# Four 64 by 64 quarters in place of full products with zero blocks, in the state-space part of a decoder layer

## Chip, cores and metric

The kernel runs on one core of one Trainium2 chip. The metric is the device time of one execution in microseconds (us), as the median of the runs.

## What is computed

One layer of a hybrid decoder for 264 columns: 256 prompt tokens and 8 sample tokens. In the mixing part, 16 attention heads and 64 state-space groups both read the same input product; their outputs are normed and go through `w_out`; a gated feed-forward part and a last gated addition follow. The change is in the state-space groups:

```
_, _, s_re, s_im = lax.associative_scan(_cplx_combine, (a_seq_re, a_seq_im, bu_re, bu_im), axis=1)
...
y = (jnp.einsum('ntgp,gcp->ntgc', s_re, prm['ssm_c_re'].astype(f32))
     - jnp.einsum('ntgp,gcp->ntgc', s_im, prm['ssm_c_im'].astype(f32))
     + prm['ssm_d'].astype(f32) * uf)
z = jnp.einsum('ntgc,gce->ntge', jax.nn.gelu(y), prm['ssm_w_glu'].astype(f32))
out = z[..., :SSM_CH_GROUP] * jax.nn.sigmoid(z[..., SSM_CH_GROUP:])
```

A group has 16 channels and a complex state of 64 numbers.

## The kernel before

**The stream.** All large weights come in units of 1024 columns (`w_load`, L336). ScalarE rounds a unit to `wh` (`w_high`, L349), VectorE forms the rest `wl` (`w_low`, L357), and TensorE makes three products of 128 by 128 by 264 columns for each block of 128 by 128: `acc<-xh,wh`, `acc<-xl,wh`, `acc<-xh,wl`. The phases are, in order: `in` (the input product), `oa` and `os` (the attention's and the state-space half of `w_out`), `pp`, `gu`, `dn`, `pg` (`stream`, L1519). The attention (`attn`, L544) and the state-space groups are worked off while `in` and `oa` are streamed; `os` needs the normed state-space output, and nothing of the stream may go ahead of it.

**Attention.** Eight steps of two heads: scores `s<-kt,q`, reductions on VectorE, exponentials and scaling on ScalarE, transposes `pt<-ident,s`, copies `ptt`, product `o<-ptt,vnat`, copies `aops` and squares `sqa`, sum `ssq_a`. `ps_a` is the product that adds up `ssq_a` for the norm (`attn_norm`, L704).

**State space.** The 64 groups are worked in 8 eighths `e` of 4 pairs `g`, with the pair's two groups `h` in the two halves of 64 partitions. Time is cut into 32 blocks of 8 tokens: inside a block the effect of the input is a product with a table `T`, and from block to block a scan runs. For each eighth:

- `ssm_x` (L950) forms tables, `px`, `ph`, `p2`, and sends `t7` through DRAM (`td`) into `T`.
- `ssm_w` (L1015) makes `pw` (8 products, 64 columns of the array each) for the scan and `py<-T,U` (8 of the same kind), which opens the sums in the bank `py`. Then `ws`, transposes `pw<-ident,ws`, copies `wt`, and on VectorE `rt`, the scan `rsh`, and the state `SB`.
- `SB` has, for each pair and each of real and imaginary part, a 128 by 128 square: group 0 in rows and columns 0 to 63, group 1 in 64 to 127, zeros in the other two quarters.
- `ssm_y` (L1098) adds the state's part, `py<-G,SB`: 4 pairs times 2 parts, 8 full products of 128 by 128 with the zeros, into `py`. Then the gelu `gy`, four transposes `py<-ident,gy`, a copy `yt`, and the transfer `ys` to DRAM.
- `ssm_glu` (L1127), eight times: transfers `wg` and `gt`, products `zb` and `za` (the gated product), `sg`, `so`, `sops` and the sum of squares `ssq_s`. There is one buffer of `gt` and `wg`. `ps_s` (`ssm_norm`, L1167) adds up `ssq_s` and stands ahead of the `os` products.

**What sets the order.** A planner (`Pace`, L76) runs all these steps as generators with costs in us and counted buffers ("+bk:2" takes two banks of `bk`), and records them in the order that it finds; up to the `os` phase a scheduler of the framework orders the instructions of each engine again. An engine then works in its fixed order. There are 8 PSUM banks: 3, later 2, are for `acc`, the others are `bk`. `py` holds one from `ssm_w` to `ssm_y`.

Every float32 product is two records in the trace. `mm` is L285, transposes are L289, ScalarE's instructions L281, DMA issues L296.

Of the kernel before, what the change touches and what calls it, by code (L numbers as in the profile page):

```python
# [12 lines left out]
ACTF = mybir.ActivationFunctionType  # L13
# [3 lines left out]
P = 128  # L17
D = 2048
KD = D // P
T = 264  # L20
# [177 lines left out]
def build(nc, tc, ctx, a):  # L198
    pace = Pace()
    V, S, G, PE, SP = nc.vector, nc.scalar, nc.gpsimd, nc.tensor, nc.sync  # L200

    def size(ap):
        n = 1
        for x in ap.shape[1:]:
            n *= x
        return n
# [17 lines left out]
    def mul(out, in0, in1):  # L224
        tt(out, in0, in1, ALU.mult)

    def add(out, in0, in1):
        tt(out, in0, in1, ALU.add)

    def sub(out, in0, in1):  # L230
        tt(out, in0, in1, ALU.subtract)
# [29 lines left out]
    def pcopy(out, in_, scale=None):  # L261
        pace.use("pool", 0.5 + 1.0e-3 * size(out))
        if scale is None:
            G.tensor_copy(out=out, in_=in_)
        else:
            G.tensor_scalar(out=out, in0=in_, scalar1=scale, scalar2=None, op0=ALU.mult)
# [5 lines left out]
    def act(out, in_, func=ACTF.Copy, **kw):  # L272
        own = {ACTF.Exp: 1, ACTF.Tanh: 1, ACTF.Gelu_apprx_tanh: 2, ACTF.Sigmoid: 3, ACTF.Silu: 4,
               ACTF.Abs_reciprocal_sqrt: 5}.get(func)
        if own and own != pace.table and not (func == ACTF.Tanh and pace.table in (1, 2, 3, 4)):
            pace.table = own
            pace.use("act", 1.28)

        own = sum(hasattr(kw.get(n), "tensor") for n in ("scale", "bias", "accum_out"))
        pace.use("act", 0.09 + 0.093 * own + 0.833e-3 * size(out))  # L280
        S.activation(out=out, in_=in_, func=func, **kw)  # L281

    def mm(out, lhsT, rhs, cost, start=True, stop=True):
        pace.use("pe", cost)
        PE.matmul(out, lhsT, rhs, start=start, stop=stop)  # L285

    def tr(out, in_, ident):
        pace.use("pe", 0.11)
        PE.transpose(out, in_, ident)  # L289

    def dma(out, in_):
        n = 4.0
        for x in out.shape:
            n *= x
        pace.move(n)
        SP.dma_start(out=out, in_=in_)  # L296
# [20 lines left out]
    def bank(shape, name):  # L317
        return banks.tile(shape, F32, tag="bank", name=name)
# [610 lines left out]
    def gsl(e):  # L929
        return slice(4 * e, 4 * e + 4)  # L930

    XT, HG, PY = {}, {}, {}
# [82 lines left out]
    def ssm_w(e):  # L1015
        q, hf = e // 2, e % 2
        u = U2[e % 2]
        gs = slice(4 * hf, 4 * hf + 4)
        yield "sp", [f"us{q}", f"us{q + 4}"] + ([f"U{e - 2}"] if e > 1 else ["c_zero"])
        for h in range(2):  # L1020
            c = q + 4 * h
            dma(u[:, 4 * h:4 * h + 4, :], us[c].rearrange("j c g k -> (j c) g k")[:, gs, :])
        yield "pe", [f"XT{e}", f"T{e}", "+bk:2"]
        pw = bank([P, 4, P], "pw")
        xt = XT.pop(e)
        for g in range(4):
            for h in range(2):
                mm(pw[64 * h:64 * h + 64, g, :], u[:, 4 * h + g, :], xt[:, g, h].rearrange("p r q -> p (r q)"), 0.11)
        pace.sig(f"Wpe{e}", "pe")

        py = bank([P, 4, P], "py")
        PY[e] = py
        Tm = T2[e % NT2]
        for g in range(4):
            for h in range(2):
                o = 16 * (2 * g + h)
                mm(py[64 * h:64 * h + 64, g, :], u[:, 4 * h + g, :], Tm[:, :, o:o + 16], 0.11, start=(g == 0), stop=False)
        pace.sig(f"U{e}", "pe")
        yield "act", "+ws"
        ws = ph1.tile([P, 4, P], F32, tag="ws", bufs=1, name="ws")  # L1040
        act(ws, pw)
        pace.rel("bk")
        yield "pe", "+bk"
        p2 = bank([P, 4, P], "pw2")
        for g in range(4):
            tr(p2[:, g, :], ws[:, g, :], ident)
        pace.rel("ws")
        yield "act", ["+wt", "as0"]
        wt = ph1.tile([P, 2, 4, 41], F32, tag="wt", name="wt")
        for h in range(2):  # L1050
            for ri in range(2):
                act(wt[64 * h:64 * h + 64, ri], p2[64 * ri:64 * ri + 64, :, 64 * h:64 * h + 41])
        pace.rel("bk")
        yield "dve", [f"rho{e}", "rot2"]
        C2, S2 = ct[:, gsl(e), :].unsqueeze(1).to_broadcast([P, 2, 4, 32]), st2[:, :, gsl(e), :]
        t1, t2, sh = rt1, rt2, rsh
        mul(t1, C2, wt[:, :, :, 0:32])
        mul(t2, S2, wt[:, ::-1, :, 0:32])
        add(t1, t1, t2)
        pace.use("dve", 0.6)  # L1060
        fl = "p r g k -> p (r g k)"
        V.tensor_tensor_scan(out=sh.rearrange(fl), data0=rho.rearrange(fl), data1=t1.rearrange(fl),
                             initial=0.0, op0=ALU.mult, op1=ALU.add)
        pace.sig(f"scan{e}", "dve")
        yield "dve", [f"Y{e - 1}", f"fst{e - 1}"] if e else ["c_zero"]
        SB = SB2[0]
        mul(t1, C2, sh)
        mul(t2, S2, sh[:, ::-1])
        for h in range(2):
            r = slice(64 * h, 64 * h + 64)  # L1070
            sub(SB[r, :, :, 64 * h + 1:64 * h + 33], t1[r], t2[r])
        pace.sig(f"S{e}", "dve")
        yield "dve"
        add(as0[:, :, gsl(e), :], as0[:, :, gsl(e), :], wt[:, :, :, 33:41])
        pace.rel("wt")
        pace.sig(f"sd{e}", "dve")
        yield "pool"
        for h in range(2):
            r = slice(64 * h, 64 * h + 64)
            pcopy(fst[r, :, gsl(e)], SB[r, :, :, 64 * h + 32])  # L1080
        pace.sig(f"fst{e}", "pool")
# [16 lines left out]
    def ssm_y(e):  # L1098
        q, hf = e // 2, e % 2
        SB = SB2[0]  # L1100
        gs = slice(4 * hf, 4 * hf + 4)
        yield "pe", [f"G{e}", f"S{e}", f"SS{e}"]
        g_, py = HG.pop(e), PY.pop(e)
        for g in range(4):
            for ri in range(2):
                mm(py[:, g, :], SB[:, ri, g, :], g_[:, ri, g].rearrange("p i c -> p (i c)"), 0.22,
                   start=False, stop=(g == 3 and ri == 1))
        pace.sig(f"Y{e}", "pe")
        yield "act", "+ws"
        gy = ph1.tile([P, 4, P], F32, tag="ws", bufs=1, name="gy")  # L1110
        act(gy, py, ACTF.Gelu_apprx_tanh)
        pace.rel("bk")
        yield "pe", "+bk"
        p2 = bank([P, 4, P], "py2")
        for g in range(4):
            tr(p2[:, g, :], gy[:, g, :], ident)
        pace.rel("ws")
        yield "act", "+yt"
        yt = ph1.tile([P, 4, P], F32, tag="yt", name="yt")
        act(yt, p2)  # L1120
        pace.rel("bk")
        yield "sp"
        dma(ys[q].rearrange("r c g h k -> (r c) g (h k)")[:, gs, :], yt)
        pace.sig(f"ys{q}{hf}", "sp")
        pace.rel("yt")
# [295 lines left out]
    with ExitStack() as order:  # L1421
# [20 lines left out]
        for e in range(8):  # L1442
            pace.add(ssm_w(e), prio=PRIO["w"])
            pace.add(ssm_y(e), prio=PRIO["y"])
            pace.add(ssm_side(e), prio=PRIO["w"])
# [289 lines left out]
```

## Time and profile before

| what | us |
|---|---|
| median of 3 runs | 1193.55 (1192.99 to 1193.68) |
| the profiled execution | 1193.6 |
| its span in the profile | 1191.5 |
| TensorE (PE) busy | 1175.1 (99%) |
| VectorE (DVE) busy | 746.1 (63%) |
| ScalarE (ACT) busy | 576.6 (48%) |

A row of the timeline has the start, the duration, the engine and operation, and out<-in by the program's names; records of the same kind that follow each other are merged, with their count. Consecutive products overlap, so that the distance of two starts is what a product costs, not its duration. "[0.92 <-...]" is idle time of the engine before the row, and what ended it.

### The profile page before, as it was taken

To read this page: it belongs to the slowest core of one execution; us is meant where nothing else is said; L and a number is where in the kernel's file an instruction comes from. 1 tells how busy PE (TensorE), PEld (TensorE's weight loads), DVE (VectorE), ACT (ScalarE), POOL (GpSimd) and SP (SyncE) were. 2 spreads that over 40 slices of the span, in tenths; PEclk is the share of its full clock that TensorE was granted. 3 is DMA by queue.
4 is the path that set the end of the run, shared out by engine and by line. 5 is a ranking of instruction groups with operands and counts; after the bars stand their busy time and mean duration, and the time that the engine had idled before them with its cause. 6 is when DMAs were issued, how large, how long until landed. Compare 5 with 4: busy or idle time off the path is not lost.

```text
span 1191.5 us, 23764 instructions
## 1 busy us (share of the span) xinstructions
PE 1175.1 (99%) x9657; PEld 1147.6 (96%) x9657; DVE 746.1 (63%) x1316; ACT 576.6 (48%) x901; POOL 56.1 (5%) x96
## 2 busy tenths in 40 slices
PE   8999999999999999999999999999999999999998
PEld 7789898899999999999999999999999999999998
DVE  8887888768896555555555555555444444446864
ACT  6276667555655444444444444444333443345542
POOL 2014232100000000000000000000000000000000
PEclk9999999999999999999999999999999999999999
DMA  8765656676675555555666555566655555666683
GB/s 276 240 194 165 169 179 178 174 211 224 213 254 178 183 178 179 188 183 178 182 183 183 180 183 186 178 180 190 251 178 179 181 185 181 179 181 215 204 251 111
DMA packets 102052, 228.93 MB, mean 192 GB/s; under 512 B 26711, under 2 KB 50359, under 8 KB 101431
## 3 DMA queue, kind: packets, MB, share of 16 engines
q1 hardware_dynamic: 101943, 227.43, 61.1%
q8 instruction: 75, 1.23, 0.4%
q14 instruction: 34, 0.28, 0.1%
HBM read 214.60 MB, written 12.80 MB: 191 GB/s over the span
## 4 chain that ended last, share of the span: by engine, by line
PE 85%; DVE 7%; DMA 4%; ACT 2%; issue 1%; SPq 1%; POOL 0%; DVEq 0%; ACTq 0%
PE acc L285 81%; PE py L285 1%; DMA T<-td 1%; DVE wl L222 1%; SPq L296 1%; DMA gt<-ys 1%; DMA ys<-yt 1%; DVE rt L222 1%; ACT s L281 1%; DVE X L222 1%; DVE G L222 0%; DMA xr<-in_x 0%; DVE ssq_x L222 0%; DVE xl L222 0%; ACT wt L281 0%
## 5 line engine op out<-in xcount | busy, mean ns | idle before, releaser
L222 DVE TENSOR_TENSOR wl<-raw,wh 128x1024 fp32r<-128x1024 f32 x354 | 432.9, 1223 | 303.7 <-PE acc L285 277.5
L281 ACT ACTIVATE wh<-raw 128x1024 fp32r<-128x1024 f32 x354 | 375.4, 1061 | 439.5 <-PE acc L285 426.5
L285 PE MATMUL acc<-hh,wh 128*128 128x264 f32 x1408 | 399.6, 284 | 0.1
L285 PE MATMUL acc<-hh,wl 128*128 128x264 f32 x1408 | 398.5, 283 | 0.0
L285 PE MATMUL acc<-hl,wh 128*128 128x264 f32 x1408 | 398.3, 283 | 0.2 <-DVE hl L236 0.2
L285 PEld LDWEIGHTS acc<-hh,wh 128*128 128x128 f32 x1408 | 265.2, 188 | 0.3 <-ACT hh L281 0.3
L285 PEld LDWEIGHTS acc<-hl,wh 128*128 128x128 f32 x1408 | 265.0, 188 | 0.4 <-DVE hl L236 0.4
L285 PEld LDWEIGHTS acc<-hh,wl 128*128 128x128 f32 x1408 | 264.0, 188 | 0.0
L285 PE MATMUL acc<-f,wh 128*128 128x264 f32 x1408 | 256.8, 284 | 0.0
L285 PEld LDWEIGHTS acc<-f,wh 128*128 128x128 f32 x1408 | 217.8, 188 | 0.1
L285 PE MATMUL acc<-f,wl 128*128 128x264 f32 x704 | 199.7, 284 | 0.0
L285 PEld LDWEIGHTS acc<-f,wl 128*128 128x128 f32 x704 | 132.5, 188 | 0.0
L285 PE MATMUL acc<-x2h,wh 128*128 128x264 f32 x256 | 72.7, 285 | 0.0
L285 PE MATMUL acc<-x2h,wl 128*128 128x264 f32 x256 | 72.5, 284 | 0.0
L285 PE MATMUL acc<-x2l,wh 128*128 128x264 f32 x256 | 71.9, 284 | 0.2 <-DVE x2l L222 0.2
L285 PE MATMUL acc<-xt,raw 128*128 128x264 f32 x224 | 51.9, 389 | 2.1 <-ACT xt L281 2.1
L285 PE MATMUL acc<-xh,wh 128*128 128x264 f32 x176 | 53.6, 305 | 0.0
L285 PEld LDWEIGHTS acc<-xt,raw 128*128 128x128 f32 x224 | 41.9, 190 | 10.7 <-ACT xt L281 3.0
L222 DVE TENSOR_TENSOR uu<-acc,Rf 128x264 f32<-128x264 f32 x44 | 19.0, 433 | 50.7 <-PE acc L285 50.7
L285 PE MATMUL acc<-xl,wh 128*128 128x264 f32 x176 | 50.1, 285 | 0.0
L285 PE MATMUL acc<-xh,wl 128*128 128x264 f32 x176 | 50.0, 284 | 0.0
L285 PE MATMUL acc<-aops,wh 128*128 128x264 f32 x256 | 49.1, 291 | 0.0
(323 smaller groups left out, 1346.1 us busy)
## 6 DMA issues: line engine op xcount, KB each, us to landing
raw<-in_w SPq DMA_DIRECT2D x367, 512.0 KB, 3.6
T<-td SPq DMA_DIRECT2D x8, 512.0 KB, 4.6
xs<-in_x SPq DMA_DIRECT2D x2, 1056.0 KB, 6.6
ppd<-ppt SPq DMA_DIRECT2D x16, 132.0 KB, 3.9
x1d<-oo SPq DMA_DIRECT2D x4, 528.0 KB, 5.4
x<-x1d SPq DMA_DIRECT2D x2, 1056.0 KB, 7.9
ppr<-ppd SPq DMA_DIRECT2D x16, 132.0 KB, 3.7
xtab<-in_xtab SPq DMA_DIRECT2D x8, 256.0 KB, 2.9
```

The lines of the kernel that those rows point to most:

```text
L222: V.tensor_tensor(out=out, in0=in0, in1=in1, op=op)
L281: S.activation(out=out, in_=in_, func=func, **kw)
L285: PE.matmul(out, lhsT, rhs, start=start, stop=stop)
L296: SP.dma_start(out=out, in_=in_)
```

## The change

The two zero quarters are left out. A pair's state part is 4 products of 64 by 64 (two groups, two parts). A group's product reads rows of its own half `k`. For the even pairs (`g` 0 and 2) the result goes to the same half of the columns, `r` = 0 for group 0; for the odd pairs (1 and 3) to the other half. So with an even and an odd pair all four quarters of the array have products. Even and odd pairs have a bank each, `py[0]` and `py[1]`. `py<-T,U` writes with the same exchange of halves. The gelu reads the two banks in two instructions, and the copy `yt` puts the odd pairs' halves back in a second instruction. `ssm_w` takes three banks in place of two, and the planner has 0.06 for a product instead of 0.22.

```
-        yield "pe", [f"XT{e}", f"T{e}", "+bk:2"]
+        yield "pe", [f"XT{e}", f"T{e}", "+bk:3"]
...
-        py = bank([P, 4, P], "py")
+        py = [bank([P, 2, P], f"py{i}") for i in range(2)]
...
-                mm(py[64 * h:64 * h + 64, g, :], u[:, 4 * h + g, :], Tm[:, :, o:o + 16], 0.11, start=(g == 0), stop=False)
+                r = 64 * (h ^ (g % 2))
+                mm(py[g % 2][r:r + 64, g // 2, :], u[:, 4 * h + g, :], Tm[:, :, o:o + 16], 0.11, start=(g < 2), stop=False)
...
-        for g in range(4):
+        for g in (0, 2):
             for ri in range(2):
-                mm(py[:, g, :], SB[:, ri, g, :], g_[:, ri, g].rearrange("p i c -> p (i c)"), 0.22,
-                   start=False, stop=(g == 3 and ri == 1))
+                for gg in (g, g + 1):
+                    for h in range(2):
+                        k, r = slice(64 * h, 64 * h + 64), 64 * (h ^ (gg % 2))
+                        mm(py[gg % 2][r:r + 64, g // 2, :], SB[k, ri, gg, k], g_[k, ri, gg].rearrange("p i c -> p (i c)"), 0.06,
+                           start=False, stop=(g == 2 and ri == 1))
...
-        act(gy, py, ACTF.Gelu_apprx_tanh)
-        pace.rel("bk")
+        for i in range(2):
+            act(gy[:, i::2, :], py[i], ACTF.Gelu_apprx_tanh)
+        pace.rel("bk", 2)
...
-        act(yt, p2)
+        act(yt[:, 0::2, :], p2[:, 0::2, :])
+        act(yt[:, 1::2, :].rearrange("p g (h k) -> p g h k", h=2), p2[:, 1::2, :].rearrange("p g (h k) -> p g h k", h=2)[:, :, ::-1, :])
```

TensorE around the state's part of the last eighth, before:

```order
L285 MATMUL acc<-aops,wl 128x264
L285 MATMUL acc<-aops,wh 128x264 x2
L285 MATMUL py<-G,SB_118 128x128 x8
L285 MATMUL acc<-aops,wl 128x264
L285 MATMUL acc<-aops,wh 128x264 x2
```

and with the change:

```order
L285 MATMUL acc<-aops,wl 128x264
L285 MATMUL py_3205<-G,SB_118 64x128
L285 MATMUL py_3206<-G,SB_118 64x128
L285 MATMUL py_3205<-G,SB_118 64x128
L285 MATMUL py_3206<-G,SB_118 64x128
L285 MATMUL py_3205<-G,SB_118 64x128 x2
L285 MATMUL py_3206<-G,SB_118 64x128 x2
L285 MATMUL py_3205<-G,SB_118 64x128 x2
L285 MATMUL py_3206<-G,SB_118 64x128 x2
...
L285 MATMUL acc<-aops,wh 128x264 x2
```

Eight products have become sixteen into two banks (the pair of rows left out is like the two above it). Between this block and `ps_s` stand 199 accumulations before, and 129 now.

TensorE where the `os` products (`acc<-sops`) begin, before:

```order
L285 MATMUL acc<-aops,wh 128x264 x2
L285 MATMUL acc<-aops,wl 128x264
L285 MATMUL ps_s<-ssq_s,onesh 128x264
L285 MATMUL acc<-sops,wh 128x264 x2
L285 MATMUL acc<-sops,wl 128x264
```

and with the change:

```order
L285 MATMUL acc<-aops,wh 128x264 x2
L285 MATMUL acc<-aops,wl 128x264
L285 MATMUL zb<-gt,wg 128x264
L285 MATMUL za<-gt,wg 128x264
L285 MATMUL ps_s<-ssq_s,onesh 128x264
L285 MATMUL acc<-sops,wh 128x264 x2
L285 MATMUL acc<-sops,wl 128x264
```

The last gated product stood 28 rows ahead of `ps_s`, and now stands right ahead of it.

TensorE at the end of the attention, with the change; `ps_a` stood, before, right behind a `py<-G,SB_118 128x128 x8`:

```order
L285 MATMUL acc<-xh,wl 128x264
L285 MATMUL o<-ptt,vnat 64x256 x2
L285 MATMUL o<-ptt,vnat 64x128 x2
L285 MATMUL ps_a<-ssq_a,onesh 128x264
L285 MATMUL pw<-XT,U_117 64x128 x8
```

The last head's `o` and the norm's product have come together.

## Rows read from the trace of the kernel before

**Rows 1.** The page: busy us, share of the span, instructions
```profile
PE 1175.1 (99%) x9657; PEld 1147.6 (96%) x9657; DVE 746.1 (63%) x1316; ACT 576.6 (48%) x901; POOL 56.1 (5%) x96
```
**Rows 2.** TensorE by stretches: length, busy (instructions), clock, DMA share, GB/s
```profile
64.00:245.00 181.00, 174.60 (x1597) 1.00 0.59 174
...
400.00:1100.00 700.00, 699.77 (x5776) 1.00 0.59 186
```
**Rows 3.** TensorE's waits: waiting<-releaser, us in total, times, longest
```profile
PE py L289 <- ACT gy L281: 1.9, 1, 1.9
```
**Rows 4.** Tile py: count, duration ns min/median/max, first and last start
```profile
L285 PEld LDWEIGHTS py<-T,U x128: 132/137/137, 60.2 to 222.2; 128*64 128x64 f32 x128
...
L285 PE MATMUL py<-G,SB x128: 273/275/377, 80.3 to 236.6; 128*128 128x128 f32 x128
...
L281 ACT ACTIVATE gy<-py x8: 597/598/603, 106.2 to 237.0; 128x512 f32<-128x512 f32 x8
```
**Rows 5.** Timeline of TensorE, the last eighth's state part
```profile
234.83 2.02 PE L285 MATMUL py<-G,SB 128*128 128x128 f32 x16 [0.92 <-POOL fst L264]
236.61 0.37 PE L285 MATMUL acc<-aops,wl 128*128 128x264 f32 x1
```
**Rows 6.** Timeline of TensorE, `pw` and `py<-T,U` between accumulations
```profile
175.66 0.28 PE L285 MATMUL acc<-xh,wl 128*128 128x264 f32 x1
175.88 1.09 PE L285 MATMUL pw<-XT,U 128*64 128x128 f32 x16
176.80 1.04 PE L285 MATMUL py<-T,U 128*64 128x128 f32 x16
177.77 0.39 PE L285 MATMUL acc<-xh,wh 128*128 128x264 f32 x1
178.00 0.29 PE L285 MATMUL acc<-xl,wh 128*128 128x264 f32 x1
```
**Rows 7.** Timeline of TensorE, column strips and row halves
```profile
48.22 0.66 PE L972 MATMUL ph<-X,xtab 128*32 128x128 f32 x16
48.81 0.93 PE L285 MATMUL s<-kt,q 64*128 64x128 f32 x8
49.67 0.49 PE L285 MATMUL acc<-xt,raw 128*128 128x264 f32 x1
```
**Rows 8.** Timeline of all engines, the last two gated products
```profile
249.13 0.61 PE L285 MATMUL zb<-gt,wg 128*128 128x264 f32 x2
...
250.65 1.00 SPq L296 DMA_DIRECT2D gt<-ys  x2
...
257.48 0.43 DVE L222 TENSOR_TENSOR oo<-acc,Ra 128x264 f32<-128x264 f32 x1 [1.33 <-PE acc L285]
...
257.83 1.22 DVE L222 TENSOR_TENSOR wl<-raw,wh 128x1024 fp32r<-128x1024 f32 x1
...
258.37 0.61 PE L285 MATMUL zb<-gt,wg 128*128 128x264 f32 x2
...
261.18 0.42 DVE L222 TENSOR_TENSOR ssq_s<-ssq_s,sqs 128x264 f32<-128x264 f32 x1
```
**Rows 9.** DMA issues: count, KB each, median us from issue to landing
```profile
gt<-ys SPq DMA_DIRECT2D x8, 128.0 KB, 3.7
```
**Rows 10.** Timeline of ScalarE and VectorE, the last two heads
```profile
181.79 0.84 ACT L281 ACTIVATE ptt<-pt 128x384 f32<-128x384 f32 x2
182.53 1.05 ACT L281 ACTIVATE wh<-raw 128x1024 fp32r<-128x1024 f32 x1
...
184.97 0.45 ACT L281 ACTIVATE aops<-o,head 128x256 fp32r<-128x256 f32 x1
...
186.11 0.42 DVE L222 TENSOR_TENSOR ssq_a<-ssq_a,sqa 128x256 f32<-128x256 f32 x1
```
**Rows 11.** Timeline of ScalarE and VectorE, the last eighth's state
```profile
227.00 1.23 ACT L281 ACTIVATE wt<-pw 64x164 f32<-64x164 f32 x4
...
233.82 0.87 DVE L222 TENSOR_TENSOR SB<-rt,rt 64x256 f32<-64x256 f32 x2
```

## The prediction

> **What bounds the kernel now.** I read the busy shares first, then the stretches, then the waits. TensorE is busy 99% of a span of 1191.5 us [rows 1]. By stretches it has waits before 245 us only: from 64 to 245 us it is busy 174.6 of 181 us, so it waits 6.4 us there, and from 400 to 1100 us it waits 0.2 us [rows 2]. So the time is TensorE's own work plus the waits of the first stage, and whatever the change takes off or adds before the `os` products moves everything behind them by as much. The longest of them is for the gelu of an eighth, 1.9 us [rows 3]; the other 4.5 us are shorter waits. They belong to chains over ScalarE, VectorE and the DMA queue, during which TensorE fills in accumulations of the weight stream. The clock is granted in full in every stretch, 2.4 GHz, and the waits here are too short to have changed that, so I cost no clock.
>
> **The products that become quarters.** One eighth's state part is now 8 full products. Each is two records in the trace, 128 in all for 8 eighths [rows 4]. The last one starts at 234.83 and its successor at 236.61, so 16 records take 1.78 us, 0.111 each [rows 5]. After the change there are 16 products of 64 by 64, 32 records, 8 for each quarter of the array. How quarters share time no row shows, but halves and strips do. The 16 records of `pw`, on two column halves, take 0.92 us from 175.88 to 176.80 [rows 6], which is 8 turns of 0.11 with two records in each. The 16 records of `ph` on four column strips take 0.59 us [rows 7], about 4 turns plus a change of split. The 8 records of `s`, on two row halves, take 0.86 us to the start of the accumulation behind them [rows 7], although their columns (128 and 256, two records of each on each half) would need 1.3 us one after another at the same rate. So all kinds of split run side by side. I take 8 turns of 0.109, 0.87 us for an eighth. That is 0.91 less, and for 8 eighths 7.3 us less. The bounds are 7.3 (four at once) and nothing (two at once, as the row and column halves were each seen).
>
> Here the Trainium skill speaks against the change. TensorE: Matmul & The Clock Gate, Part 3 (The mechanism) says that a weight load overlaps running products only when the row group differs. By that rule the two column halves of one row half would take turns, and the saving would be nothing. The trace does not bear it out: the column halves of `py<-T,U` have the same rows, their loads take 137 ns each [rows 4], and 16 of them fit into 0.97 us [rows 6].
>
> **What the split itself costs.** From the last accumulation ahead of `pw` to the second one behind `py<-T,U` is 175.66 to 178.00, 2.34 us [rows 6]. Two blocks of 8 turns and two ordinary accumulation steps of 0.12 would be 1.98. So entering and leaving a split costs 0.36, 0.18 each way. Full products don't pay it, the quarters do. In the printed order there are 12 more such changes than before (some quarters stand beside work that is split already), 2.2 us. TensorE's own work falls by 7.3 - 2.2 = **5.1 us**.
>
> **Operations that are added beside TensorE.** `gy` and `yt` become two instructions each. One gelu of 512 columns takes 598 ns [rows 4]; a ScalarE instruction of 256 columns takes 0.45 (`aops` [rows 10]), so two halves cost at most 0.3 more and at least nothing. I take 0.2, 8 x 2 x 0.2 = 3.2 us more for ScalarE in all. Accumulations cover that; where the chain itself is waited for it comes on top, and I leave it to the bounds below. The other order of the halves in `py<-T,U` still gives each half 8 records, so I cost it at nothing.
>
> **The waits that go and those that come.** The second bank of `py` is held from `ssm_w` to `ssm_y`, so the order of the whole first stage is another. The 6.4 us of waits [rows 2] belong to the old order, and I take them all off. For the new order I go through the places where little stands between a producer and its consumer on TensorE:
>
> - **The last gated product.** It now stands right ahead of `ps_s` and the `os` products. In the order of before `ps_s` stands 28 printed rows behind it. From `zb` to the end of `ssq_s` takes 258.37 to 261.60, 3.2 us [rows 8], and the two products themselves cover 0.9. In the new order VectorE has an `oo` and a `wl` just ahead (0.4 and 1.2 us), which delay `so` by some 0.7. So 3.0, bounds 2.3 and 3.1.
> - **The round trip to that product.** After `zb` at 249.13, the loads of the next `gt` are issued at 250.65 and take 1.0 to issue [rows 8]. They land after 3.7 us [rows 9], so the next `zb` can start 6.2 us after the first. Between the last two there are now 39 accumulations (4.8) and 0.9 of their own, 5.7. So 0.6; bounds 0 and 3.5, since the trace's own distance is 9.2 (249.13 to 258.37 [rows 8]).
> - **`ps_a`.** It stood behind an eighth's products, 22 accumulations after the last head's `o`; now it follows that `o` directly, with `pw`, `py` and the `oa` products queued behind it. From `aops` at 184.97 to the end of `ssq_a` at 186.53 is 1.6 us [rows 10], and ScalarE has a cast, a `sops` and a `wh` ahead of `aops`, which start it some 0.6 late. So 2.1, bounds 1.5 and 2.6.
> - **`ptt` of the last two heads.** Their `o` needs 0.84 us of copies [rows 10], in one of the two behind a `wh` (1.05 [rows 10]), and 6 accumulations or 4 transposes stand between. 2.1 for both, bounds 0.8 and 3.
> - **The state of the fifth and of the last eighth.** For the last one, `wt` to the end of `SB` takes 227.00 to 234.69, 7.7 us [rows 11], with two `wl` and two `oo` in it, of which the new order leaves one each: 6.2, and 0.5 for the transposes ahead. What covers it is 36 accumulations, one gated pair and those transposes, 5.7. That leaves 1.0; for the other, where the last head's score reductions stand in the chain, I take 1.1. Together 2.1, bounds 0.5 and 4.
> - **Elsewhere** (the decode softmax again, two early heads, one `T`) 2.5, bounds 1 and 5, from the 4.5 us of shorter waits that the old order has.
>
> That is 12.4 us of new waits against 6.4 old ones. **Sum:** -5.1 - 6.4 + 12.4 = +0.9 us. The profiled execution took 1193.6 us, as good as the median of the runs (1193.55), so 1194.5 us. About 0.2%, 2.4 us, is what a measurement can tell from no change: 1191.2 to 1195.9 is "the same". At its lower bounds the new waits are 6.1 (1188.2 us), at the upper ones 21 (1203); not all ends come together.
>
> **Rivals.**
> 1. *The new waits are no longer than the old.* For it: nearly all of TensorE's first stage is filler, and a wait taken early gives every later chain time to catch up, so that my terms don't simply add. Against it: the places with `ps_s` and `ps_a` have no filler at all. Then only the 5.1 us count: 1188.5 us. Chance 0.24.
> 2. *The end of the state-space chain becomes the bound* (slower). Its last stretch is serial: products of the last eighth, gelu, transposes, `ys`, `gt`, gated product, and again `gt` and gated product, in one buffer each. The last eighth's products now stand 129 accumulations ahead of `os`, where it was 199. If the round trip is not 6.2 but the 9.2 that the trace shows, the wait in front of the last gated product is 3.5 instead of 0.6, and the total 1197.4; with 2 us more on the state of an eighth, 1199.4. It decides from a round trip of 5.7 up. For it: the DMA queue issues in order, with weight loads between. Against it: in the trace of before those loads were issued nearly 8 us ahead of the `zb` at 258.37 [rows 8], so 9.2 was a distance in the order. Chance 0.26.
> 3. *The quarters don't run side by side.* The two row halves write into one bank here, the upper and the lower partitions of it, while `s` in the trace writes its row halves into two banks; no row shows the mix. If they take turns, a block is 16 turns, 1.74 us, and the saving is gone: 1194.5 + 7.0 = 1201.5 us. Chance 0.08. TensorEngine Tiling (Array Packing) in the Trainium skill, under Restrictions and Gotchas, has this as a rule: different row tiles cannot use one PSUM bank at the same time. No run shown yet tells whether partitions apart count as one bank in its sense.
>
> **How the numbers follow.** The forecast has 0.42; nearly all of it (0.39) is inside the 2.4 us, 0.01 below and 0.02 above. With rival 1 that makes 0.25 for faster, with rivals 2 and 3 0.36 for slower. The range, 1188.5 to 1199.5, takes in rivals 1 and 2 and leaves out rival 3 and the outer halves of the bounds, together 0.2. The likeliest case alone reaches from 1191 to 1198.
>
> **What would show it.** In the profile after the change: blocks of 32 `py<-G,SB` records of 0.9 us, not 1.75 (step one, rival 3); the accumulation behind each block 0.1 late (step two); a wait of TensorE for `ssq_s` at `ps_s` of 2 to 3 us and one at `ps_a` of 2 us, neither of which exists now; busy time from 64 us to `os` down by 5; and no new waits after `os` starts. Without the waits at `ps_s` and `ps_a` I am wrong by their sum, and rival 1 is right; a wait at the last `zb` of more than 2 us is rival 2.

## The result, and the profile after

The change is slower: 1201.04 us median (1200.46 to 1202.97, 4 runs) against 1193.62 us (1192.99 to 1195.09, 4 runs), a ratio of 1.0070 with a 95% interval of 1.0058 to 1.0081. (Here and below a ratio is worked out from the runs, and is not exactly the quotient of the two medians.) The forecast was 1194.5, the range ended at 1199.5.

The profiled execution took 1200.46 us, with a span of 1197.0. Its busy shares, in the form of [rows 1]:

```profile
PE 1174.9 (98%) x9785; PEld 1143.2 (96%) x9785; DVE 745.3 (62%) x1316; ACT 577.9 (48%) x917; POOL 55.1 (5%) x96
```

TensorE is as busy as before, with a span 5.5 us longer. Where that comes in is read by stretches (length, busy, instructions, granted clock, DMA share, GB/s). First the kernel before, up to 64 us, from there to its first `os` product, and the 30 us behind it:

```profile
0.00:64.00 64.00, 58.59 (x316) 1.00 0.79 257
64.00:264.25 200.25, 193.85 (x1749) 1.00 0.60 177
264.25:294.25 30.00, 30.00 (x249) 1.00 0.74 247
```

and the change, to its own first `os` product, behind that, and around two places of lower clock:

```profile
0.00:64.00 64.00, 59.27 (x322) 1.00 0.80 259
64.00:268.20 204.20, 191.47 (x1869) 0.99 0.59 176
268.20:298.20 30.00, 29.95 (x237) 0.96 0.67 221
...
189.00:190.00 1.00, 0.83 (x2) 0.50 0.97 315
190.00:191.00 1.00, 1.00 (x7) 0.50 0.99 325
191.00:192.00 1.00, 1.00 (x14) 0.50 1.15 345
...
267.00:268.00 1.00, 0.47 (x1) 0.63 0.73 262
268.00:269.00 1.00, 1.00 (x4) 0.50 0.96 215
269.00:270.00 1.00, 1.00 (x6) 0.50 0.61 161
270.00:271.00 1.00, 1.00 (x8) 0.66 0.97 389
```

Three readings. TensorE waits 204.20 - 191.47 = 12.7 us up to `os`, where it waited 6.4. It is busy 2.4 us less. And twice, for some 3 us, its clock is 1.2 GHz, which it never was before. From the first `os` product to the end of the span it now takes 1197.0 - 268.20 = 928.8 us, and took 1191.5 - 264.25 = 927.25: 1.5 us more, though nothing there was changed. So the 5.5 us are 6.3 - 2.4 up to `os` and 1.5 behind it. The cut at 64 us is a little unfair: by then the change has already done 0.7 us more (59.27 us busy, 58.59 before). Counted from the start of the span it is busy 1.7 us less and waits 5.6 us more up to `os`, so each of these two terms is good to some 0.7 us; their sum stays.

The waits of the change, in the form of [rows 3] (us in total, times, longest):

```profile
PE py L285 <- DMA T<-td: 3.3, 3, 1.6
PE ps_s L285 <- DVE ssq_s L222: 2.5, 1, 2.5
PE acc L285 <- ACT xt L281: 2.2, 2, 1.9
PE ps_a L285 <- DVE ssq_a L222: 2.1, 1, 2.1
PE sd L627 <- POOL q L540: 2.1, 1, 2.1
...
PE py L285 <- DVE SB L222: 0.9, 1, 0.9
PE o L285 <- ACT ptt L281: 0.9, 2, 0.7
```

The gelu's wait of [rows 3] is gone (0.3 is left). `ps_s` and `ps_a` stand as forecast. The largest, for the table `T` (0.8 in total before), and the one of the decode scores `sd`, were not.

The quarters themselves, an eighth between accumulations (start, duration, row):

```profile
97.57 0.28 PE L285 MATMUL acc<-xh,wl 128*128 128x264 f32 x1
97.78 1.10 PE L285 MATMUL py<-G,SB 64*64 64x128 f32 x32
98.82 0.39 PE L285 MATMUL acc<-xh,wh 128*128 128x264 f32 x1
99.04 0.28 PE L285 MATMUL acc<-xl,wh 128*128 128x264 f32 x1
```

The 32 records have 1.04 us, where the full products had 1.78 [rows 5]: four at once.

### The profile page after: what moved, and what is told of

It is laid out like the page before. It is cut to its first block, busy times and chain, and to the rows that moved or that the text cites. A ratio compares the mean times of both kernels' runs of the same rounds, so it can differ in the third digit from the quotient of the medians.

```text
span 1197.0 us, 24042 instructions
## 1 busy us (share of the span) xinstructions
PE 1174.9 (98%) x9785; PEld 1143.2 (96%) x9785; DVE 745.3 (62%) x1316; ACT 577.9 (48%) x917; POOL 55.1 (5%) x96
## 4 chain that ended last, share of the span: by engine, by line
PE 85%; DVE 8%; DMA 3%; ACT 2%; issue 1%; SPq 0%; POOL 0%; ACTq 0%; DVEq 0%; POOLq 0%
PE acc L285 81%; DMA T<-td 1%; PE py L285 1%; DVE wl L222 1%; DMA pt<-in_p 1%; ACT s L281 1%; DVE rt L222 1%; DMA td<-t 1%; DVE G L222 1%; DVE X L222 0%; DVE ssq_x L222 0%; DMA xr<-in_x 0%; DVE xl L222 0%; DVE sc L222 0%; PE o L285 0%
```

## The experiments

Each was timed beside the kernel before on the same chip (1192.68 to 1192.96 us there); a ratio is to that.

**e1_column_halves: the quarters' worth in the change's own order.** The rows of every engine stand in the same order as in the change.

```
-    mm(py[gg % 2][r:r + 64, g // 2, :], SB[k, ri, gg, k], g_[k, ri, gg]...
+    mm(py[gg % 2][r:r + 64, g // 2, :], SB[:, ri, gg, k], g_[:, ri, gg]...
```

> The changed kernel with the same 16 products, banks and order of every engine, but each product reads all 128 rows, zeros included, so that it takes a column half of the array and two run side by side in place of four. Theory (the quarters save what was forecast; the loss comes from the order that the third bank brings): each state block goes from 0.84 to about 1.7 us, 8 x 0.87 = 7.0 us more, 1208.0 (1206 to 1209.5), with the same waits. Rival (the small products themselves do the harm, by the clock or by what stands behind them): the two stretches at the lower clock go away and the time is 1201 or less.

Measured: 1208.51 us, 1.0123 (1.0106 to 1.0140). By the medians that is 7.5 us more than the change, by the two ratios 6.3 (the two were not timed beside each other). The timeline of one block:

```profile
100.76 0.28 PE L285 MATMUL acc<-xh,wl 128*128 128x264 f32 x1
100.97 1.97 PE L285 MATMUL py<-G,SB 128*64 128x128 f32 x32
102.87 0.39 PE L285 MATMUL acc<-xh,wh 128*128 128x264 f32 x1
103.09 0.28 PE L285 MATMUL acc<-xl,wh 128*128 128x264 f32 x1
```

1.90 us in place of 1.04, 0.86 for each eighth, and the waits at `ps_a` (2.1) and `ps_s` (2.6) as in the change. So four products run side by side, and in this order nearly all of the 6.9 us that they save is time. The quarters are not what makes the change slow; the lower clock was here too, without any quarter.

**e4_bank_alone: the held bank, with full products.**

```
-        yield "pe", [f"XT{e}", f"T{e}", "+bk:2"]
+        yield "pe", [f"XT{e}", f"T{e}", "+bk:3"]
...
+        py = [bank([P, 2, P], f"py{i}") for i in range(2)]
...
+        for i in range(2):
+            act(gy[:, i::2, :], py[i], ACTF.Gelu_apprx_tanh)
+        pace.rel("bk", 2)
```

> The kernel before with py in two banks, three banks taken in ssm_w, and the gelu in two halves; the full products, the planner's cost of 0.22 and the copy yt as before. Theory (the held bank is what spoils the order): px, which needs three banks, starts later from the third eighth on, the waits of the first stage grow by some 4 us, 1197 (1195 to 1200), without any quarter. Rival (the order is spoilt by the planner's lower cost or by the quarters): 1193.6, within 1.

Measured: 1200.59 us, 1.0066 (1.0053 to 1.0079). The direction held; the size was twice the expected one. The first row of its waits:

```profile
PE py L285 <- DMA T<-td: 6.7, 5, 4.0
```

The wait of 4.0 us is followed by 1.2 GHz for nearly 7 us:

```profile
225.00:226.00 1.00, 0.00 (x0) 0.77 0.98 245
226.00:232.00 6.00, 5.37 (x29) 0.50 0.20 80
232.00:233.00 1.00, 1.00 (x8) 0.82 0.00 0
```

So the bank alone costs as much as the whole change, through `T`. It is not the same loss: `ps_a` has no wait here, and `ps_s` 0.4 us. (The gelu in two instructions comes with the two banks; v4 below has it too and loses nothing.) Its timeline also has a clean block of full products, to compare with that of the quarters above:

```profile
99.15 0.28 PE L285 MATMUL acc<-xh,wl 128*128 128x264 f32 x1
99.28 1.95 PE L285 MATMUL py<-G,SB 128*128 128x128 f32 x16
100.98 0.37 PE L285 MATMUL acc<-xh,wh 128*128 128x264 f32 x1
101.19 0.28 PE L285 MATMUL acc<-xl,wh 128*128 128x264 f32 x1
```

From the accumulation ahead to the second one behind it is 101.19 - 99.15 = 2.04 us, with quarters 99.04 - 97.57 = 1.47: a block saves 0.57 when the changes of the split are paid.

**e6_cost_on_before: the planner's number alone.** The kernel before, with the same products and banks.

```
-                mm(py[:, g, :], SB[:, ri, g, :], ..., 0.22,
+                mm(py[:, g, :], SB[:, ri, g, :], ..., 0.12,
```

> The kernel before with one number changed: the planner has 0.12 for each of the 8 full products (as much as for two quarters in the changed kernel) in place of 0.22. Same products, banks and instructions; only the order differs: the last gated product stands right ahead of ps_s. Theory (any order with that pair at its end pays the wait at ps_s and the lower clock behind it): a wait of 2.5 us there, 1.5 us for the clock, about 4 us over the kernel before, ratio 1.0035 (1.001 to 1.006). Rival (the held bank alone costs, the planner's number nothing): 1.000 within 0.001.

Measured: 1204.02 us, 1.0092 (1.0077 to 1.0106): 11 us for a number that changes no instruction. The wait at `ps_s` came as expected, but the larger one is again for `T`, and behind `ps_s`, which starts at 274.5, the clock stayed at 2.4 GHz. It fell to 1.2 GHz elsewhere, for some 3 us behind a wait of 2.5 us for `T` (its waits, and two stretches):

```profile
PE py L285 <- DMA T<-td: 6.3, 5, 2.5
PE ps_s L285 <- DVE ssq_s L222: 2.6, 1, 2.6
```

```profile
275.00:278.00 3.00, 3.00 (x26) 1.00 0.88 279
234.00:239.00 5.00, 3.46 (x24) 0.66 0.74 197
```

So the theory had the place right and the size wrong: it priced the end of the stage only.

**e5_cost_only: the change, with 0.11 for a quarter in place of 0.06.**

> The changed kernel with 0.11 for a quarter in the planner, as much for two as the kernel before has for one full product; the third bank stays. The last gated product still stands right ahead of ps_s. Theory (the bank alone is enough to spoil the order): waits and clock as in the change, ratio 1.006 (1.004 to 1.009). Rival (the planner's number is what matters, as it did alone on the kernel before): 1.002 or less.

Measured: 1204.28 us, 1.0097 (1.0083 to 1.0110), above the range that was expected (1.009 at most). The rival falls: giving the planner the old number back does not help while the bank is held (the waits for `T` are 8.7 us in all here).

**e2_fill: is it the waiting that lowers the clock?** The two norm products get idle products ahead of them, 8 at `ps_a` and 10 at `ps_s`.

```
+        for _ in range({"a": 8, "s": 10}.get(name, 0)):
+            PE.matmul(ps[:, 0:128], onesd, onesd, start=True, stop=True)
```

> The changed kernel with idle products (128 columns of ones) ahead of the two norm products: 8 ahead of ps_a, 10 ahead of ps_s, where TensorE only waits. The scheduler also puts 7 of pw's 8 products ahead of ps_a and one os product ahead of ps_s. Theory (the clock falls because TensorE runs dry there): the granted clock stays at 2.4 GHz throughout; 1.5 us less at ps_s, only some 0.3 less at ps_a, since the transfer T behind it lands when it lands; together 1199.2 (1198.5 to 1200). Rival (the quarters or something else lowers the clock): both stretches stay at 1.2 GHz, 1200.5 to 1201.5.

Measured: 1200.05 us, 1.0065 (1.0052 to 1.0077). At both places the clock now stays up, and in the same execution it falls somewhere else, behind the wait at `sd`, which was 2.1 us in the change and 2.8 here:

```profile
186.00:192.00 6.00, 5.25 (x44) 1.00 0.69 208
262.00:272.00 10.00, 8.82 (x69) 1.00 0.75 196
163.00:168.00 5.00, 4.94 (x55) 0.66 0.39 137
```

So the quarters are not what lowers the clock: here it falls behind waits of TensorE, and it stays up at the two that idle products fill. In time it is inconclusive: the interval overlaps the change's. At `ps_a` little could come out, since the wait for `T` behind it grew from 1.3 to 1.9 us; at `ps_s` a wait of 1.2 us for `gt` at the last `zb` came in.

**e3_norm_later: take away the wait at `ps_s` by order.**

```
     def ssm_norm():
...
         pace.sig("op_os", "pe")
+        yield "pe", ["os_u0"]
         yield from rstd([ssq_s], onesh, R["s"], "s")
...
```

> The changed kernel with ps_s moved behind the first unit of os products (27 printed rows later), all else in the same order. Theory: the 2.5 us wait at ps_s goes, and with it the 1.5 us that the lower clock costs behind it: 1197.0 (1196 to 1198.5). Rival (the products of os wait for the last gated product just as long, or the first epilogue waits for the norm instead): 1200 to 1201.

Measured: 1203.74 us, 1.0099 (1.0085 to 1.0113), slower than the change; both expectations were wrong on where the time goes. The wait at `ps_s` is gone. TensorE runs on, and from 280.60, 12.6 us behind its first `os` product, it stands 4.15 us for `wl`, with ScalarE in front of it:

```profile
280.20 0.40 PE L285 MATMUL acc<-sops,wh 128*128 128x264 f32 x2
284.75 0.39 PE L285 MATMUL acc<-sops,wl 128*128 128x264 f32 x1 [4.15 <-DVE wl L222]
```

```profile
280.56 0.64 ACT L281 ACTIVATE ppo<-pt 128x528 fp32r<-128x528 f32 x1 [6.57 <-issue]
281.11 1.04 ACT L281 ACTIVATE wh<-raw 128x1024 fp32r<-128x1024 f32 x1
```

`ppo` needs `pt`, which SyncE issues behind two loads of `xs` of 1056 KB each, and those go out 0.07 us behind the end of the last gated product's sum (`ssq_s` ends at 270.92, `xs` goes at 270.99, `pt` at 271.84; in the change 267.48, 267.55 and 268.40). `ppo` starts at 280.56, and the next `wh` and `wl` stand behind it in their queues. In the change the same `ppo` waited too, until 278.01, while TensorE had lost the time at `ps_s` already. So the wait at `ps_s` stood for the late end of the state-space chain, and moved, it came back with a lower clock of its own. (This execution also had 1.2 GHz for ten microseconds behind `ps_a`, 190 to 200 us, where a second wait for `T` fell into the slow stretch. By this and by earlier waits for `T` its first `os` product starts only 0.24 us sooner than in the change, 267.96 for 268.20.)

**v2_sum_bank, c1_px_split, c2_sum_px_split: hold the second bank only for a moment.** In v2 the direct part of all pairs stays in one bank, the odd pairs' state part gets a bank from `ssm_y` to the gelu, and VectorE adds the two. In c1 and c2, `px` asks for two banks and then one in place of three at once; c1 is the change with that, c2 is v2 with that.

```
-        yield "pe", [f"XT{e}", f"T{e}", "+bk:3"]
+        yield "pe", [f"XT{e}", f"T{e}", "+bk:2"]
...
-        yield "pe", [f"G{e}", f"S{e}", f"SS{e}"]
+        yield "pe", [f"G{e}", f"S{e}", f"SS{e}", "+bk"]
...
+        copy(gy[:, 1::2, :], py[1])
+        add(gy[:, 1::2, :], gy[:, 1::2, :], py[2])
```

> Quarters, but ssm_w takes two banks as before: the direct part of all four pairs goes into one bank; the second bank is taken only in ssm_y, for the odd pairs' state part, and VectorE adds it to the odd pairs' direct part (a copy and an addition of 128x256) ahead of their gelu. Theory (holding the third bank from ssm_w on is what delays the next eighths): px starts as early as before, the last eighth's products 70 printed rows earlier than in the change; but the last gated product still stands right ahead of ps_s, with its wait and clock, so about the kernel before, ratio 1.000 (0.998 to 1.003). Rival (the two operations on VectorE lengthen the chain as much as the bank did): 1.005 or more.

> The changed kernel, and ssm_x takes two banks for px and a third for ph separately. Theory (the bank that py holds, not the size of px's request, delays the chain): the last eighth's products stand where they stood in the change (901 rows, 895 there), the last gated product right ahead of ps_s, ratio 1.006 (1.004 to 1.009). Rival (three banks at once are what px starves for): 1.002 or less.

> As v2_sum_bank, and ssm_x takes two banks for px and a third for ph separately, in place of three at once. The last gated product now stands 36 rows ahead of ps_s (39 in the kernel before), and ps_a 18 rows behind the last head. Theory: without a wait at either norm product the 3.4 us that TensorE's own work is shorter by come out, ratio 0.997 (0.995 to 0.999), clock 1.000. Rival (every new order of the first stage brings its own waits of several us, whatever the banks): 1.001 to 1.005.

Measured: v2 1200.07 us, 1.0050 (1.0036 to 1.0064); c1 1201.74 us, 1.0069 (1.0056 to 1.0083); c2 1193.15 us, 1.0000 (0.9991 to 1.0008). c1 came as expected: while `py` holds the bank, the size of `px`'s request is nothing. v2 gave the last `px` nearly its old time (209 us, 207.9 before) and was still 6 to 7 us slower, which meets its rival's mark (1.005). It waits for `T` and at `ps_s` much as the change does, and at two places more:

```profile
PE zb L285 <- DMA gt<-ys: 3.1, 1, 3.1
PE py L285 <- DMA T<-td: 3.0, 3, 1.5
PE otd L289 <- ACT ods L281: 2.4, 1, 2.4
PE ps_s L285 <- DVE ssq_s L222: 2.2, 1, 2.2
```

c2, with the last gated product 36 rows ahead of `ps_s`, is at the level of the kernel before; the expected gain did not come out (1.0000, 0.999 was the upper end). It has v2's two operations on VectorE as well, so these alone are not what v2 lost by.

**v4_old_plan and v6_glu1: the planner's order of before.** The odd pairs' state part goes into the bank that the transposes of `gy` take anyway, VectorE adds it, and for v4 the planner counts the banks and the products' time as before. v6 has 0.09 for a quarter in place of 0.11, and a higher priority for the gated products.

```
+        p2 = bank([P, 4, P], "py2")
...
+                        mm((p2 if gg % 2 else py)[r:r + 64, gg, :], SB[k, ri, gg, k], ..., 0.11,
```

> Quarters under the planner's order of the kernel before: same counted banks, 0.11 for a quarter; the odd pairs' state part goes into the bank that the transposes of gy use later, and VectorE adds it (a copy and an addition of 128x256) ahead of the gelu. Only the scheduler behind the planner moves rows. The last gated product stands 15 rows ahead of ps_s (39 before), ps_a 39 behind the last head. Theory: the shorter work (3.4 us) comes out, less some 1 us of wait at ps_s without a lower clock: ratio 0.998 (0.9955 to 1.001). Rival (every new order costs several us): 1.003 or more.

> As v4_old_plan, with the planner's cost of a quarter at 0.09 and its priority of the gated products raised by one step. The last gated product stands 39 rows ahead of ps_s, as in the kernel before, the last eighth's products at row 820 (825 before). Theory: no wait at ps_s, none at ps_a beyond 1 us, the shorter work comes out: ratio 0.997 (0.995 to 1.000), clock 1.000. Rival (every new order costs several us): 1.003 or more.

Measured: v4 1192.83 us, 0.9998 (0.9989 to 1.0007); v6 1191.65 us, 0.9991 (0.9982 to 1.0000), about 1.1 us faster than the kernel before, at the edge of what the interval can tell, and the fastest here. Both lie inside their ranges, but v4 at no gain and v6 at a third of the expected one. v6's stretch up to `os`:

```profile
64.00:261.86 197.86, 191.75 (x1870) 0.99 0.60 178
```

It waits 6.1 us, where the kernel before waited 6.4, and is busy 2.1 us less.

**e7_v6_column_halves: what the quarters are worth in that order.** The edit is that of e1, the order of every engine that of v6.

> v6_glu1 with the same order of every engine, but each of the 16 products reads all 128 rows, zeros included, and takes a column half: two side by side in place of four, as e1_column_halves is to the change. Theory (four at once saves 0.86 us for an eighth wherever TensorE bounds): 8 x 0.86 = 6.9 us more than v6_glu1, ratio 1.005 to the kernel before (1.003 to 1.007), so that this order without the saving is slower than the kernel before. Rival (v6_glu1 gained by its order alone): 1.001 or less.

Measured: 1193.64 us, 1.0010 (1.0001 to 1.0019): 2.0 us more than v6 (2.3 by the ratios), not 6.9.

```profile
64.00:264.45 200.45, 196.06 (x1871) 1.00 0.61 176
```

Up to `os` TensorE is busy 4.3 us longer than in v6 and waits 1.7 us less (4.4 in place of 6.1). v6 also runs some 3 us at 1.2 GHz, behind a wait of 1.95 us for `SB`; this kernel does not, though it has that wait too (1.98 us). So in an order where the other chains are close, more than half of the shorter work comes back as waits and clock; in the change's order (e1) nothing did. The theory's 6.9 us was wrong. The time meets the rival's mark (1.001), but the rival's reading does not hold either: without the quarters this order is no faster than the kernel before. Up to `os` it waits 2.0 us less than that and is busy 2.2 us longer.

## Why the prediction was wrong, by its own steps

- **The quarters: right.** Four run at once, and rival 3 is out: 0.84 us from the first record to the last, 1.04 to the next product. The rule behind rival 3 (the Trainium skill, TensorEngine Tiling (Array Packing), Restrictions and Gotchas), taken bank by bank, does not hold here: both row halves write into one bank, in different partitions of it, at the same time. The Trainium skill's PSUM — Partial Sum Buffer, in "PSUM bank collisions raise a hardware error", quotes the wider rule too, but states it from measurements for bank and group of partitions together, and the 0.84 us agree with that. Four quarters in one bank, which would need no third bank, were not tried: there two row halves would write the same partitions of one bank. That loads overlap only where the row group differs (the Trainium skill, TensorE: Matmul & The Clock Gate, Part 3) the trace contradicts again, since two quarters of one half of rows run together: in the block above the four products of a turn start within 0.02 us of one another.
- **The price of the split: nearly right.** 0.91 less 0.36 is 0.55 for a block that stands alone, and 0.57 was measured. But all eight pay a change on both sides, the one behind `ph`, which is split too, as well: 8 x 0.57 = 4.6, not 5.1. That is an estimate, since four of the eight blocks of the kernel before stood beside split rows and paid changes of their own. With the 0.9 of the next sentence and the 1.4 of slow clock below, it comes close to the 2.4 us by which TensorE is busy less (1.7 from the start of the span). The prediction had named 5 as a sign. Two of the blocks ran 0.45 us longer, since their first two products start when one half of `SB` is written and the others wait for the other half.
- **The new waits named: right or too high.** `ps_s` 2.5 (forecast 3.0), `ps_a` 2.1 (2.1), `ptt` 0.9 (2.1), the last round trip none (0.6), the state of an eighth 0.9 and the two times 0.45 inside blocks (2.1). Rival 2 did not come.
- **"Elsewhere" failed.** It was put at 2.5 us, at most 5, from the size of the old order's short waits. Measured: 12.7 us less the ones above (2.5, 2.1, 0.9, 0.9) is 6.3, of which `T` has 3.3 and `sd` 2.1. The terms went through the places where rows had moved together; none asked for the start of the chain. `px` of the last eighth started at 207.90 before and at 224.20 with the change; `px` needs three banks, and `py` now held one more. From `px` a table goes over ScalarE, VectorE and two transfers into `T`, and TensorE ends up waiting for it. In e4 and e6, with full products, the waits for `T` come to 6.7 and 6.3 us. How much of the delay of `px` is the bank's is not shown: the last one starts at 212.24 with the bank alone (e4) and at 221.93 without it (e6). Nor does a late `px` cost by itself: in v4 it starts at 215.30, and v4 is no slower than the kernel before.
- **"So I cost no clock" failed.** It was true of the waits in the trace of before and was carried over to new waits as long as 2 to 3 us. Half of the slow busy time is lost: 1.4 us of 2.8 behind `ps_a`, and 1.5 behind `ps_s`. What the first of these cost is open, because the wait for `T` behind it ended with a transfer; the second cost its 1.5 us.

In sum, to the +0.9 that was forecast come: elsewhere +3.8, clock +2.9, the split +0.5, the other waits -2.6 together. That makes +5.5, as the span has it. The total of the waits came out as forecast, 12.7 us for 12.4, and that was luck: "elsewhere" was too low by about as much as the named ones were too high. So the sum went wrong in TensorE's own work: 5.1 us less was forecast, and 2.4 less up to `os` with 1.5 more behind it came, which is 0.9 less. Of these 4.2 us the clock, costed at nothing, has 2.9. The profiled execution has another 1.4 us outside its span (3.5, where it was 2.1), which the trace does not explain, and the median lies 0.6 above it. The other three executions of the change had longer spans (1198.7, 1198.7 and 1201.0) and less outside them, so part of the usual loss is in no trace.

That the order loses the time and not the quarters is shown by e1 and v4. That the held bank alone can bring an order as costly is shown by e4; that it is not the only thing that can, by e6 and v2. Which of the change's inputs made which of its waits stays open, since e4 has next to nothing of the two norm waits, and e6 has the one at `ps_s` without a second bank. How the scheduler comes from a shorter number to a later `px` is not shown by any run.

## What to carry to other kernels

Where a planner sets the order, every edit that it can see (a bank, a cost, a priority) is a new order of the whole stage, and here that is worth up to 11 us, more than the edit itself could save. So change the work and keep the planner's inputs at first (v4, which did, lost nothing, though it gained nothing either), and when you price a new order, follow each chain from its first step (when does it get its buffers?) and not only the places where rows have moved together. A wait that stands in front of a stage may stand for something late behind it; taken away by order alone, it comes back further on. And work taken off the busiest engine is time only as far as the chains beside it keep up: the same edit was worth some 7 us in one order and 2 in another.

## What was not expected of the hardware

- Behind many waits of 2 us and more the granted clock fell from 2.4 to 1.2 GHz: behind 2.5 at `ps_s` in the change, 2.8 at `sd` in e2, 4.0 at `T` in e4. It did not behind 2.1 at `sd` in the change, 2.6 at `ps_s` in e6 or 2.9 at `T` in e5, so the length of the wait alone does not decide it; of two like waits for `SB`, 1.95 us in v6 and 1.98 in e7, it fell behind the first only. The slow stretch lasted some 3 us in most cases, nearly 7 in e4 and c1, and 10 in e3 and v2; in c1, e3 and v2 a further wait fell into it.
- A change of the split costs more on the way out than on the way in: the quarters start 0.21 us after the accumulation ahead (0.13 for full products in e4), and the next accumulation follows the last quarter record by 0.20 (98.62 to 98.82), where it followed the last full one by 0.03.
